# A two-layer decoder trunk on one core: a reordered opening, and softmax over a block's eight heads one block behind the scores

## The chip, the cores and the metric

The kernel runs on one core of one Trainium2 chip, in one launch. The metric is device time in microseconds (us), the median of several runs. The engines are TensorE (PE, matrix products, with PEld for its weight loads), VectorE (DVE), ScalarE (ACT), GpSimd (POOL) and SyncE (SP), on whose queue most DMAs are issued.

## What is computed

Two layers, each with a token mixer and a dense feed-forward part, on 1024 tokens of width 1024, in float32. The mixer projects to queries (8 heads of 64), keys and values (2 heads) and a pooling branch; attention looks at the own block of 128 tokens and the one before, with a sink per head:

```python
mod = c_act @ ada_w[l] + ada_b[l]                       # shift, scale, gate of both halves
h = rms_norm(x, g_pre_mix[l]) * (1.0 + scale_m) + shift_m
proj = h @ w_in[l] + b_in[l]                            # q 512, k 128, v 128, u 512 columns
...
k_cat = jnp.concatenate([jnp.pad(kb, pad)[:, :-1], kb], axis=2)    # previous block, own block
scores = jnp.einsum("bnqkgd,bnskd->bnkgqs", qb, k_cat) * (HEAD_DIM ** -0.5)
valid = (diff[None] >= 0) & (diff[None] < WINDOW) & (key_abs >= 0)
scores = jnp.where(valid[None, :, None, None], scores, NEG_INF)
probs = jax.nn.softmax(jnp.concatenate([scores, sink], axis=-1), axis=-1)[..., :-1]
out = jnp.einsum("bnkgqs,bnskd->bnqkgd", probs, v_cat)
...
mix = jnp.concatenate([attn_out, pool_out], axis=-1) @ w_out[l]
x = x + gate_m * rms_norm(mix, g_post_mix[l])
# then h = modulated rms_norm(x); x = x + gate_f * rms_norm((silu(h @ w_gate) * (h @ w_up)) @ w_down)
```

Block 0 has no block before it: the half of its scores that falls there is masked.

## The kernel before, in words

Every float32 operand of a dense product is split into a high and a low part (`split`: ACT casts the high part, L215; DVE subtracts for the low part, L216), and a product is three PE products (`mm3`, L255, L258, L259): high by high, high by low, low by high. Tokens are worked in two halves of 512 (four tiles of 128). The tile framework's planner sets each engine's order from the order of issue, the dependences and its own costs; `after` adds an order on one engine. `run` interleaves generators step by step: a main stream of dense work and streams beside it.

The opening, layer 0, half 0: x is loaded on SP's queue; the scale and shift columns of the first norm come from `ada_w[0]` in four blocks of two k (a k is 128 columns of the model width). Block 0 is a product of PE with one row as result (`ada_first_row`, L355); blocks 1 to 3 are eight weighted sums on DVE each (`ada_first_sum`, L346, L348). `ada_first_ab` (L364, L370) turns a sum into columns; `first_pieces` transposes the normalised x (L519), scales and shifts on ACT (L512) and splits. `q_pass` (four accumulator banks, 12 products of 512 columns per k) and `kv_pass` (12 of 256 per k) consume the pieces k by k. The mean squares are made on ACT (L476), the reciprocal root in small DVE steps (L266 to L273). The rotary tables are made on DVE after the last sums (L196 to L207).

Attention, `attention(h, ...)`, is a generator that runs beside the dense work (half 0 beside the u, key/value and query passes of half 1; half 1 beside the output projection of half 0 and the u pass). A group is one key head of one block (four query heads). Per group: `att_queries` (split, four transposes L798, copy L803), `att_scores` twice (four products L813, L814; two masked maxima on DVE, L816), `att_softmax` (four short DVE steps L828, L831, L836, L837; four exponentials L835 on ACT; three scalings on DVE, L841, one on ACT, L843), `att_probs` twice (four transposes L851 and a split), `att_values` twice. A group's softmax comes after the next group's queries; its probabilities come between the next group's scores. Score tiles are two (tag sb), each for one group. Beside all this runs a stream of ada weights (`ada_sum`, L287, L289, two `ar` buffers) for the rest of the layer's modulation.

Of the kernel before, what the change touches and what calls it, by code (L numbers as in the profile page):

```python
# [11 lines left out]
F32 = mybir.dt.float32  # L12
# [8 lines left out]
P = 128  # L21
# [21 lines left out]
HALO = 16  # L43
EPS = 1e-6
# [21 lines left out]
def hybrid_decoder_kernel(  # L66
# [36 lines left out]
        mix=dict(cfa=2, cfb=2, qkv=6, bqkv=1, uT=4, pt=2, vz=5, rt=1, qT=1, pth=2, pwh=1, pwl=1),  # L103
# [38 lines left out]
    make_identity(nc, eye)  # L142
    ones_r = const.tile([P, 1], F32R, name="ones_r")
# [4 lines left out]
    nc.vector.tensor_copy(ident_r, eye)  # L148
# [10 lines left out]
    mask = const.tile([P, 2, 2 * P], F32, name="mask")  # L159
    nc.gpsimd.memset(mask, 0.0)  # L160
    fill = NEG / SCALE
    for i in range(2):
        nc.gpsimd.affine_select(
            out=mask[:, i, :], in_=mask[:, i, :], pattern=[[-1, 2 * P]], compare_op=ALU.is_ge,
            fill=fill, base=P, channel_multiplier=1,
        )
        nc.gpsimd.affine_select(
            out=mask[:, i, :], in_=mask[:, i, :], pattern=[[1, 2 * P]], compare_op=ALU.is_gt,
            fill=fill, base=0, channel_multiplier=-1,
        )  # L170
    nc.gpsimd.memset(mask[:, 0, 0:P], fill)
# [4 lines left out]
    for g, w in enumerate(WINDOWS):  # L176
        nc.vector.tensor_scalar(rcnt[:, g, :], tpos, float(w), None, op0=ALU.min)
    nc.vector.reciprocal(rcnt, rcnt)


    nc.sync.dma_start(c_raw, c[0].rearrange("(p j) -> p j", j=KD))
    nc.scalar.activation(c_act, c_raw, AF.Silu)


    NB = S // P
    pos_i = const.tile([P, NB], I32, name="pos_i")
    nc.gpsimd.dma_start(pos_i, positions[0].rearrange("(t p) -> p t", p=P))
# [7 lines left out]
    def rotary_tables(prev):  # L195
        after(nc.vector.tensor_copy(pos_f, pos_i), prev)  # L196
# [7 lines left out]
        nc.vector.tensor_scalar(ang, ang, math.pi, -math.pi, op0=ALU.min, op1=ALU.max)  # L204
        nc.scalar.activation(sin_t, ang, AF.Sin)
        nc.vector.scalar_tensor_tensor(cos_t, ang, -1.0, ang, op0=ALU.mult, op1=ALU.max)
        nc.vector.tensor_scalar(cos_t, cos_t, -1.0, math.pi / 2.0, op0=ALU.mult, op1=ALU.add)  # L207
        nc.scalar.activation(cos_t, cos_t, AF.Sin)
# [4 lines left out]
    def split(hi, lo, src):  # L213

        nc.scalar.activation(hi, src, AF.Copy)  # L215
        recent["split"] = nc.vector.tensor_sub(lo, src, hi.bitcast(F32))  # L216
# [44 lines left out]
    def rsqrt_mean(ss, n):  # L261
# [8 lines left out]
        for _ in range(3):  # L270
            nc.vector.scalar_tensor_tensor(z, y, -0.5, a, op0=ALU.mult, op1=ALU.mult)
            nc.vector.tensor_mul(z, z, y)
            nc.vector.scalar_tensor_tensor(y, z, 1.5, y, op0=ALU.add, op1=ALU.mult)  # L273
# [36 lines left out]
    def load_cols(l):  # L310
        rows = t_("rows", [P, P])[:NROW]
        r = 0
        for src, n in (
# [3 lines left out]
            (nc.sync if l else nc.scalar).dma_start(rows[r : r + n, :], src.rearrange("(r p) -> r p", p=P))  # L317
            r += n
        bank = msc_bank()
# [5 lines left out]
    CW = 2 * P  # L325

    def ada_first_load(n0):

        src = ada_w[0].rearrange("(p j) n -> p j n", j=KD)
        tags = {0: ("cfa",) * 2, 1: ("cfb",) * 2, 2: ("sa", "sa", "sb", "sb"), 3: ("cfa",) * 2}[n0 // CW]  # L330
        nj = KD // len(tags)
        ws = []
        for i, tag in enumerate(tags):
            w = t_(tag, [P, nj, 2, CW])
            for m, part in enumerate((1, 0)):
                c0 = part * D + n0
                nc.sync.dma_start(w[:, :, m, :], src[:, i * nj : (i + 1) * nj, c0 : c0 + CW])
            ws += [w[:, j].rearrange("p m n -> p (m n)") for j in range(nj)]
        return ws

    def ada_first_sum(acc, ws, js):

        for j in js:
# [3 lines left out]
            else:  # L347
                last = nc.vector.scalar_tensor_tensor(acc, ws[j], c_, acc, op0=ALU.mult, op1=ALU.add)  # L348
        return last

    def ada_first_row(ws):

        bank = msc_bank()
# [1219 lines left out]
```

## Time and profile before

| | |
|---|---|
| median of three runs | 1914.03 us (1912.49 to 1915.56) |
| the profiled execution, its own time | 1912.51 us |
| its span, first to last instruction | 1910.7 us |
| mean granted TensorE clock | 0.997 |
| HBM read and written | 267.25 and 72.89 MB |

The page's first part gives each engine's busy time; a busy PE is not PE at its peak, so a window's busy time is set against its length and against the number of records. A line of a timeline gives start, length (of all records that it merges), engine, line, operation, what it writes and reads, and in brackets how long the engine stood idle before it and what released it. A group line gives busy time and mean ns of one, then the idle time before its instructions.

### The profile page before, as it was taken

What the parts mean: (1) busy time and instruction counts of PE and PEld (TensorE: products, weight loads), DVE (VectorE), ACT (ScalarE), POOL (GpSimd) and SP (SyncE); (2) the same over time, 40 slices, a digit from 0 to 9 for tenths busy, and PEclk for the clock granted to TensorE, in tenths of its full rate; (3) what the DMA queues carried; (4) which work ended last, traced back from release to release, by engine and by line L of the source; (5) the groups of instructions that cost most, each with busy time, mean ns of one, the idle gap of its engine ahead of it and who ended that gap; (6) DMA issues with size and microseconds to landing.
All of it is one profiled execution on the core that took longest, in us unless ns stands there. A gap on an engine that the chain in (4) does not pass through costs nothing.

```text
span 1910.7 us, 26084 instructions
## 1 busy us (share of the span) xinstructions
PE 1866.3 (98%) x8978; PEld 1539.2 (81%) x8978; DVE 1545.1 (81%) x2898; ACT 950.5 (50%) x1789; POOL 26.8 (1%) x84
## 2 busy tenths in 40 slices
PE   6999999999999999999999989999999999999997
PEld 4887788888888888888888868888888887888886
DVE  5999886668898888788879998846889888877687
ACT  4876795653222223445548667845622222244452
POOL 1000000000000000000000000000000000000000
PEclk9999999999999999999999999999999999999999
DMA  9355563555655665944554464536654565574342
GB/s 324 115 155 153 163 226 122 186 177 183 204 179 189 208 207 178 323 137 145 183 168 128 133 183 165 177 110 208 215 188 150 198 209 202 197 252 150 115 152 102
DMA packets 227428, 341.86 MB, mean 179 GB/s; under 512 B 16952, under 2 KB 124360, under 8 KB 227296
## 3 DMA queue, kind: packets, MB, share of 16 engines
q1 hardware_dynamic: 227152, 340.17, 54.2%
q8 instruction: 70, 1.15, 0.2%
q14 instruction: 62, 0.51, 0.1%
q0 software_dynamic: 32, 0.00, 0.0%
q10 hardware_dynamic: 112, 0.04, 0.0%
HBM read 267.25 MB, written 72.89 MB: 178 GB/s over the span
## 4 chain that ended last, share of the span: by engine, by line
PE 79%; DVE 11%; DMA 5%; ACT 3%; issue 1%; SPq 0%; DVEq 0%; ACTq 0%
PE acc L255 24%; PE acc L258 24%; PE acc L259 24%; DMA ar<-in_ada_w_dram 2%; DVE lo L216 2%; DVE ada L289 2%; PE msc L851 1%; PE msc L519 1%; ACT hi L215 1%; DMA raw<-in_w_up_dram 1%; PE pv L255 1%; DVE ph L216 1%; DMA ar<-x 1%; DVE sb L816 1%; PE pv L258 1%
## 5 line engine op out<-in xcount | busy, mean ns | idle before, releaser
L215 ACT ACTIVATE hi<-raw 128x1024 fp32r<-128x1024 f32 (+1 forms) x388 | 332.4, 869 | 365.8 <-PE acc L258 196.2
L216 DVE TENSOR_TENSOR lo<-raw,hi 128x1024 fp32r<-128x1024 f32 (+1 forms) x388 | 380.0, 986 | 123.6 <-ACT hi L215 122.8
L255 PE MATMUL acc<-t,hi 128*128 128x512 f32 x704 | 274.6, 390 | 1.5 <-ACT hi L215 1.5
L258 PE MATMUL acc<-t,hi 128*128 128x512 f32 x704 | 274.0, 389 | 0.0
L259 PE MATMUL acc<-t,lo 128*128 128x512 f32 x704 | 271.9, 389 | 0.0
L255 PE MATMUL acc<-bh,hi 128*128 128x512 f32 x520 | 202.8, 390 | 0.0
L259 PE MATMUL acc<-bh,lo 128*128 128x512 f32 x520 | 202.4, 389 | 0.0
L255 PE MATMUL acc<-hT,hi 128*128 128x512 f32 x480 | 189.7, 395 | 0.6 <-DVE fn L638 0.6
L258 PE MATMUL acc<-hT,hi 128*128 128x512 f32 x480 | 188.4, 392 | 0.0
L259 PE MATMUL acc<-hT,lo 128*128 128x512 f32 x480 | 187.7, 392 | 0.0
L1107 DVE TENSOR_TENSOR fn<-acc,fn 128x512 f32<-128x512 f32 x220 | 150.2, 683 | 37.4 <-PE acc L259 37.4
L255 PEld LDWEIGHTS acc<-t,hi 128*128 128x128 f32 x704 | 132.2, 188 | 30.8 <-ACT hi L215 3.9
L259 PEld LDWEIGHTS acc<-t,lo 128*128 128x128 f32 x704 | 132.2, 188 | 29.0 <-DVE lo L216 1.5
L258 PEld LDWEIGHTS acc<-t,hi 128*128 128x128 f32 x704 | 132.2, 188 | 27.2
L258 PE MATMUL acc<-ph,hi 128*128 128x512 f32 x320 | 124.6, 389 | 0.0
L1043 ACT ACTIVATE fn<-fn 128x512 f32<-128x512 f32 x44 | 27.8, 633 | 180.3 <-DVE fn L1107 180.3
L289 DVE SCALAR_TENSOR_TENSOR ada<-ar,c_act,ada 128x512 f32<-128x512 f32 x140 | 104.6, 747 | 12.0 <-DMA ar<-in_ada_w_dram 11.0
L259 PEld LDWEIGHTS acc<-bh,lo 128*128 128x128 f32 x520 | 97.6, 188 | 20.4
L255 PEld LDWEIGHTS acc<-bh,hi 128*128 128x128 f32 x520 | 97.6, 188 | 20.0
L255 PEld LDWEIGHTS acc<-hT,hi 128*128 128x128 f32 x480 | 90.2, 188 | 18.9 <-DVE fn L638 1.4
L259 PEld LDWEIGHTS acc<-hT,lo 128*128 128x128 f32 x480 | 90.1, 188 | 18.2
L255 PE MATMUL acc<-hi 128*128 128x512 f32 x256 | 101.1, 400 | 2.8 <-DVE fn L638 1.6
(315 smaller groups left out, 3834.6 us busy)
## 6 DMA issues: line engine op xcount, KB each, us to landing
ar<-in_ada_w_dram SPq DMA_DIRECT2D x160, 256.0 KB
raw<-in_w_gate_dram SPq DMA_DIRECT2D x44, 512.0 KB
raw<-in_w_up_dram SPq DMA_DIRECT2D x44, 512.0 KB
raw<-in_w_in_dram SPq DMA_DIRECT2D x80, 256.0 KB
raw<-keeps SPq DMA_DIRECT2D x40, 512.0 KB
keeps<-fn SPq DMA_DIRECT2D x66, 256.0 KB
two_b<-in_w_down_dram SPq DMA_DIRECT2D x30, 512.0 KB
raw<-keepa SPq DMA_DIRECT2D x25, 512.0 KB
```

Of the source, the lines that this page charges most:

```text
L215: nc.scalar.activation(hi, src, AF.Copy)
L216: recent["split"] = nc.vector.tensor_sub(lo, src, hi.bitcast(F32))
L255: ins = nc.tensor.matmul(dst, lh, rh, start=first, stop=False)
L258: nc.tensor.matmul(dst, lh, rl, start=False, stop=False)
L259: return nc.tensor.matmul(dst, ll, rh, start=False, stop=last)
L289: ins = nc.vector.scalar_tensor_tensor(acc, w, c_act[:, i : i + 1], acc, op0=ALU.mult, op1=ALU.add)
L519: ins = nc.tensor.transpose(bank[:, t * P : (t + 1) * P], src[t], ident)
L816: nc.vector.tensor_tensor_reduce(out=s[:, ii, :], in0=bank[:, ii * 2 * P : (ii + 1) * 2 * P], in1=mask[:, min(blk, 1), :], scale=SCALE, sc ...
L851: nc.tensor.transpose(bank[:, i * P : (i + 1) * P], s[:, ii, ck * P : (ck + 1) * P], ident)
L1043: nc.scalar.activation(g, g, AF.Silu)
L1107: nc.vector.tensor_add(halves_of(dst)[m], bank, halves_of(src)[m])
```

## The change

The opening: x is loaded by four DMAs on ACT's queue ahead of the ada weights; the row and position loads move, too. The ada blocks are now of 1, 1, 2, 2 and 2 k (`FIRST_BLOCKS`); the first two are row products on PE, the others sums on DVE. Half of the mean squares are made on DVE. x is scaled in three pieces of columns (128, 128, 768), each with an order behind named instructions. The rotary angles and the counts of the pool are made on DVE before the mean squares; only the two sines stay behind. The second block's pieces are issued in the middle of the first query products.

Attention: softmax is made for the eight heads of a block at once, in two steps (exponentials; scalings), after the next block's keys; scores go to three tiles in turn; probabilities come between the next block's scores, group by group. For block 0 scores, softmax, probabilities and values leave out the 128 columns of the missing block, and the cleared keys and values of it go. Buffers: qkv 5 instead of 6, pth 1 instead of 2, vz 6 instead of 5. In the dense work of half 1 the query pass comes before key/value.

```diff
-        mix=dict(cfa=2, cfb=2, qkv=6, bqkv=1, uT=4, pt=2, vz=5, rt=1, qT=1, pth=2, pwh=1, pwl=1),
+        mix=dict(cfa=2, cfb=2, qkv=5, bqkv=1, uT=4, pt=2, vz=6, rt=1, qT=1, pth=1, pwh=1, pwl=1, sc=1),
...
+    x0 = []
+    for t in range(NT):
+        x0.append(t_("fn", [P, D]))
+        nc.scalar.dma_start(x0[t], x[0, t * P : (t + 1) * P, :])
     nc.scalar.activation(c_act, c_raw, AF.Silu)
...
+    FIRST_BLOCKS = (
+        (0, 1, ("cfa",), 4), (1, 1, ("cfa",), 4), (2, 2, ("cfb",) * 2, 4),
+        (4, 2, ("sa", "sa", "sb", "sb"), 2), (6, 2, ("cfa",) * 2, 4),
+    )
...
+    def square_sum_v(ss, t, i, src, junk):
+        ins = nc.vector.tensor_tensor_reduce(
+            out=junk, in0=src, in1=src, scale=1.0, scalar=0.0, op0=ALU.mult, op1=ALU.add,
+            accum_out=ss[:, 2 * t + i : 2 * t + i + 1],
+        )
+        after(ins, ident_made)
...
-    def q_pass(l, hT, par, qkvs, ask):
+    def q_pass(l, hT, par, qkvs, ask, first=None):
...
                 mm3(banks[t], hi[:, tiles[t]], lo[:, tiles[t]], wh, wl, k == 0, k == KD - 1)
+                if first and k == 0 and t == 1:
+                    first()
...
+    def att_seen(blk):
+
+        return slice(0 if blk else P, 2 * P)
...
-    def att_softmax(n, sts, mx, nsink):
...
+    def att_softmax(blk, sts, mx, nsink):
+
+        nm = t_("st", [P, 8])
+        es = t_("st", [P, 8])
+        sm = t_("st", [P, 8])
+        nc.vector.scalar_tensor_tensor(nm, mx, -1.0, nsink, op0=ALU.mult, op1=ALU.min)
+        nc.vector.tensor_sub(es, nm, nsink)
         nc.scalar.activation(es, es, AF.Exp)
...
+        seen = [sts[i // 2][:, i % 2, att_seen(blk)] for i in range(NH)]
+        for i, sl in enumerate(seen):
             nc.scalar.activation(sl, sl, AF.Exp, bias=nm[:, i : i + 1], accum_out=sm[:, i : i + 1])
+        yield
         nc.vector.tensor_add(es, es, sm)
         nc.vector.reciprocal(es, es)
...
+        for i, sl in enumerate(seen):
+            if i % GRP < GRP - 1:
                 nc.vector.tensor_scalar(sl, sl, es[:, i : i + 1], None, op0=ALU.mult)
             else:
                 nc.scalar.activation(sl, sl, AF.Copy, scale=es[:, i : i + 1])
...
+        for t in range(NT + 1):
             cur = None
...
             if prev:
-                pblk, pt, pn, sts, mx = prev
-                att_softmax(pn, sts, mx, nsink)
-                yield
-            for u in range(GRP // 2):
+                pblk, pt, psts, pmx = prev
+                yield from att_softmax(pblk, psts, pmx, nsink)
+            for n in range(NKV):
                 if cur:
...
+                    qT = att_queries(n, qkvs[t])
+                    both = t_(("sb", "sb", "sc")[count % 3], [P, GRP // 2, 2, 2 * P])
+                    count += 1
+                    yield
+                for u in range(GRP // 2):
+                    if cur:
+                        cur[2].append(both[:, u])
+                        att_scores(blk, n, u, qT, cur[3], both[:, u])
+                    flush()
+                    if prev:
+                        late.append((pblk, n, u, att_probs(pblk, psts[n * GRP // 2 + u]), cat, pt))
+                    yield
...
     acc = ada_first_row(wss[0])
...
+    rotary_angles()
+    rstd = stats(xs, t_("rs", [P, 8]), junk=t_("pth", [P, 512]))
+    FIRST_COLS = (slice(0, P), slice(P, 2 * P), slice(2 * P, D))
+    scaled = normalise(xs, rstd, cs=FIRST_COLS[0], hold=(recent["row"], recent["hot"]))
...
     first_pieces(0)
+    acc = ada_first_row(wss[1])
...
+    queries0 = q_pass(0, hts[0], par, qkvs0, ask_q, second_piece)
+    normalise(xs, rstd, cs=FIRST_COLS[1], hold=recent["hold"])
...
+            if b == 0:
+                normalise(xs, rstd, cs=FIRST_COLS[2], hold=rest)
+            elif b + 1 < NB0:
+                last = ada_first_sum(acc, wss[b + 1], range(KD * i // nk, KD * (i + 1) // nk))
...
             yield from u_pass(l, 0, hts[0], cols, uts[0], piece_read, ask)
+            yield from q_pass(l, pieces, par, qkvs[1], ask)
             yield from kv_pass(l, pieces, par, qkvs[1], ask)
-            yield from q_pass(l, pieces, par, qkvs[1], ask)
```

## Rows read from the trace of the kernel before

**Rows 1.** The page: busy time, share of the span and instructions of each engine; then the chain of work that ended last, by engine.

```profile
PE 1866.3 (98%) x8978; PEld 1539.2 (81%) x8978; DVE 1545.1 (81%) x2898; ACT 950.5 (50%) x1789; POOL 26.8 (1%) x84
...
PE 79%; DVE 11%; DMA 5%; ACT 3%; issue 1%; SPq 0%; DVEq 0%; ACTq 0%
```

**Rows 2.** The windows: stretch, its length, busy time and records of PE, PEld, DVE, ACT and POOL, granted clock, DMA share, GB/s.

```profile
0.00:27.20 27.20, 12.42 (x37) 3.90 (x37) 9.13 (x36) 13.30 (x27) 5.12 (x21) 1.00 0.97 319
27.20:60.00 32.80, 32.72 (x198) 28.82 (x199) 29.63 (x70) 18.49 (x39) 3.54 (x6) 1.00 0.79 270
60.00:100.00 40.00, 40.00 (x241) 33.74 (x240) 37.22 (x127) 32.03 (x73) 0.27 (x2) 1.00 0.35 101
100.00:215.00 115.00, 109.75 (x643) 90.94 (x642) 109.08 (x299) 80.18 (x207) 2.86 (x12) 1.00 0.56 165
215.00:290.00 75.00, 73.12 (x420) 61.06 (x419) 63.79 (x184) 66.06 (x159) 2.80 (x8) 1.00 0.56 186
290.00:1010.00 720.00, 718.93 (x3271) 594.65 (x3270) 574.58 (x848) 306.69 (x478) 5.06 (x13) 1.00 0.56 185
1010.00:1050.00 40.00, 38.38 (x252) 32.92 (x251) 36.50 (x104) 34.49 (x84) 2.00 (x7) 1.00 0.48 145
1050.00:1165.00 115.00, 109.29 (x606) 89.78 (x605) 102.67 (x285) 75.27 (x192) 3.03 (x9) 0.99 0.53 158
1165.00:1230.00 65.00, 63.43 (x371) 53.66 (x371) 56.09 (x161) 59.09 (x142) 2.15 (x6) 1.00 0.54 183
1230.00:1900.00 670.00, 668.09 (x2955) 549.73 (x2953) 519.16 (x761) 263.83 (x396) 0.00 (x0) 1.00 0.52 175
```

**Rows 3.** The chain of work that ended last, from 100 to 215 us, by line.

```profile
by line: DMA ar<-in_ada_w_dram 20.1%; DVE ada L289 12.6%; DVE lo L216 7.1%; DMA raw<-in_w_in_dram 5.6%; PE acc L258 5.1%; PE acc L259 4.7%; PE acc L255 4.3%; DVE sb L816 3.9%; DVE ph L216 3.8%; DVE pt L947 3.2%; PE msc L851 2.3%; issue 2.3%
```

**Rows 4.** The waits of PE from 100 to 215 us: what waited for what, us in total, times, longest.

```profile
PE msc L774 <- DVE hi L769: 2.1, 1, 2.1
PE msc L387 <- ACT ph L215: 0.5, 1, 0.5
```

**Rows 5.** The timeline of the opening: start, length, engine, line, operation, in brackets the idle time before and its releaser.

```profile
10.53 0.63 ACT L476 ACTIVATE junk<-fn 128x512 bf16<-128x512 f32 x1 [0.55 <-DMA fn<-in_x_dram]
...
13.61 9.38 PE L355 MATMUL msc<-cfa,c_act 128*1 128x512 f32 x16 [6.72 <-DMA cfa<-in_ada_w_dram]
...
14.41 2.19 ACT L503 ACTIVATE fn<-fn,rs 128x1024 f32<-128x1024 f32 x2 [2.40 <-DVE rs L273]
...
22.92 0.66 PE L519 MATMUL msc<-ident,fn 128*128 128x128 f32 x4
...
23.67 1.05 PE L364 MATMUL msc<-ones_r,ar 1*128 1x1 f32 x8
...
25.20 1.45 ACT L512 ACTIVATE uT<-msc,colp 128x512 f32<-128x512 f32 x2 [1.59 <-DVE colp L375]
...
27.22 0.50 PE L255 MATMUL acc<-hi,hT 128*128 128x512 f32 x1 [1.47 <-ACT hT L215]
```

**Rows 6.** The windows again (columns as in rows 2), around the row product of the opening and around 1138 us. The clock column has no record of the time before 18.4 us and prints 1.00 there.

```profile
13.60:18.30 4.70, 4.69 (x6) 0.72 (x7) 2.65 (x7) 3.36 (x4) 0.00 (x0) 1.00 1.09 369
18.40:23.00 4.60, 4.60 (x12) 0.83 (x11) 0.70 (x2) 0.00 (x0) 0.00 (x0) 1.00 1.10 353
1133.00:1137.90 4.90, 2.69 (x11) 1.26 (x9) 4.90 (x9) 3.02 (x6) 0.00 (x0) 1.00 0.48 150
1138.00:1141.30 3.30, 3.20 (x8) 2.52 (x9) 3.14 (x10) 2.28 (x9) 0.00 (x0) 0.50 0.55 161
```

**Rows 7.** The timelines of PE and DVE from 33 to 57 us: the columns of the second ada block, the first dense products of k=2, two weighted sums, and the first and last step of the rotary angles.

```profile
33.68 0.95 PE L364 MATMUL msc<-ones_r,ar 128*128 128x1 f32 x8
...
37.66 1.19 PE L255 MATMUL acc<-hi,hT 128*128 128x512 f32 x4
...
42.22 1.54 DVE L348 SCALAR_TENSOR_TENSOR ar<-cfa,c_act,ar 128x512 f32<-128x512 f32 x2
...
51.41 0.16 DVE L196 CAST pos_f<-pos_i 128x8 f32<-128x8 int32 x1
...
56.31 0.20 DVE L207 TENSOR_SCALAR cos_t<-cos_t 128x64 f32<-128x64 f32 x1
```

**Rows 8.** The DMA issues of the first 100 us: the positions, KB, median us from issue to landing.

```profile
pos_i<-in_positions_dram POOLq DMA_DIRECT2D x1, 4.0 KB, 7.3
```

**Rows 9.** The timeline of PE: two score products of block 0, one behind the other.

```profile
73.81 0.28 PE L813 MATMUL msc<-sa,qT 128*128 128x256 f32 x1
73.93 0.28 PE L814 MATMUL msc<-sa,qT 128*128 128x256 f32 x1
```

**Rows 10.** The whole chain in order of time: start, length, what, number. Seven probability transposes.

```profile
288.31 0.77 PE msc L851 x7
```

**Rows 11.** The groups of DVE and of ACT from 64 to 215 us, shapes kept apart: busy us of all, mean ns of one, idle us before them and what ended it.

```profile
L816 DVE CUSTOM_DVE_ANT_0 sb<-msc,mask 128x256 f32<-128x256 f32 x44 | 17.2, 414 | 0.5 <-PE msc L814 0.2
...
L216 DVE TENSOR_TENSOR ph<-msc,pth 128x512 fp32r<-128x512 f32 x19 | 13.0, 685 | 1.0 <-ACT pth L215 0.9
...
L828 DVE SCALAR_TENSOR_TENSOR st<-st,sk 128x4 f32<-128x4 f32 x11 | 1.7, 154 | 0.0
...
L835 ACT ACTIVATE sb<-sb,st 128x256 f32<-128x256 f32 x44 | 21.8, 503 | 1.1 <-DVE st L828 1.1
...
L215 ACT ACTIVATE hi<-raw 128x512 fp32r<-128x512 f32 x31 | 19.1, 631 | 4.0 <-issue 2.1 <-PE acc L259 1.6 <-PE acc L258 0.4
```

More of the change, by code (lines that the diff above doesn't have):

```diff
@@ L43 @@
 HALO = 16
+UW = 576
 EPS = 1e-6
@@ L142, in hybrid_decoder_kernel @@
     make_identity(nc, eye)
+    NB = S // P
+    pos_i = const.tile([P, NB], I32, name="pos_i")
+    nc.gpsimd.dma_start(pos_i, positions[0].rearrange("(t p) -> p t", p=P))
     ones_r = const.tile([P, 1], F32R, name="ones_r")
@@ L333, in ada_first_load @@
         for i, tag in enumerate(tags):
[L334 to L337, printed above, removed]
+            w = t_(tag, [P, nj, 2, cw])
+            for j in range(0, nj, step):
+                for m, part in enumerate((1, 0)):
+                    c0 = part * D + k0 * P
+                    nc.sync.dma_start(
+                        w[:, j : j + step, m, :], src[:, i * nj + j : i * nj + j + step, c0 : c0 + cw]
+                    )
             ws += [w[:, j].rearrange("p m n -> p (m n)") for j in range(nj)]
@@ L348, in ada_first_sum, with ada_first_ab @@
                 last = nc.vector.scalar_tensor_tensor(acc, ws[j], c_, acc, op0=ALU.mult, op1=ALU.add)
+            after(last, recent["summed"])
+            recent["summed"] = last
         return last
     def ada_first_row(ws):
[L353 to L363 removed]
+        bank = msc_bank()[0:1, : ws[0].shape[1]]
+        for j in range(KD):
+            nc.tensor.matmul(bank, c_act[:, j : j + 1], ws[j], start=j == 0, stop=j == KD - 1)
+        row = t_("ar", [P, 512])[0:1, : ws[0].shape[1]]
+        recent["row"] = nc.scalar.activation(row, bank, AF.Copy)
+        return row
+    def ada_first_ab(b, acc, cols, ab):
+        k0, nk = FIRST_BLOCKS[b][:2]
+        bank = msc_bank()
+        for i in range(2 * nk):
             nc.tensor.matmul(
@@ L864, in att_values @@
         ph, pl = probs
-        for ck in range(2):
+        first = 0 if blk else 1
+        for ck in range(first, 2):
             vh, vl = attn["v", blk - 1 + ck]
@@ L868, in att_values @@
             cs = slice(ck * 2 * P, (ck + 1) * 2 * P)
-            opening = n == 0 and u == 0 and ck == 0
+            opening = n == 0 and u == 0 and ck == first
             closing = n == NKV - 1 and u == 1 and ck == 1
@@ L1357, in hybrid_decoder_kernel @@
                 layer_rows(0, par)
-        if b + 1 < NB0:
+        if 0 < b < NB0 - 1:
             first_pieces(b + 1)
-        next(keys0)
+        if (k0 + nk) % 2 == 0:
+            next(keys0)
     normalise(xs1, rstd1)
-    rotary_tables(last)
+    rotary_tables(recent["cast"])
     def ada_jobs(l):
```

238 lines of the change are left out of this document (109 added, 129 removed).

## The prediction

> **What bounds the kernel now.** I read the page first. TensorE (PE) is busy for 98% of the span, and the chain that ended last is 79% PE [rows 1]: to gain, the change must take work from PE or close gaps on it. Next come the windows [rows 2], in which PE's busy time is set against each stretch. The gaps stand in two places. In the first 27.2 us PE is busy for 12.4, and none of that is the dense work that the rest of the time consists of. In the four stretches with attention (100 to 290 and 1010 to 1230) it falls short by 5.25, 1.88, 1.62, 5.71 and 1.57 us, 16.0 together. From 27 to 100 and in the 1390 us of the other stretches it falls short by 3.1 us. In the two stretches with the large shortfall VectorE (DVE) is busy for 109.1 and 102.7 of 115 us, and the chain of the first runs through the stream of ada weights (its DMA 20.1%, its sums 12.6%) [rows 3]: in them DVE and that stream set the pace. The largest single waits of PE there are for DVE's key split (2.1 us) [rows 4].
>
> The opening is read from its timeline [rows 5]. The last quarter of x is squared from 10.53; the first ada block lands by 13.61, and PE then makes its row product (L355) in 16 records until 22.9; transposes, the columns (L364), ACT's scaling and the cast follow, and the first dense product runs at 27.22. DMA is at 0.97 of its time and 319 GB/s until then [rows 2]: bytes, not issue, decide when things land.
>
> **Part 1, the opening.** Before the first row product the kernel loads x (2.1 MB) and an ada block of 2.1 MB; the new block is 1.05 MB. 4.3 MB at 319 GB/s are 13.5 us, as seen [rows 5]; 3.2 MB are 10 us, with a start of about 1 us 11. x now goes by ACT's queue beside the ada block on SP's; both share the same bandwidth, so I let both land at 11. The row product has half the columns: 16 records that take 0.43 us each at the low pace and 0.21 at the high one. In the trace 6 records of 512 columns took 4.70 us first and 12 took 4.60 later [rows 6], so the pace doubles about 4.7 us after PE begins. Here that leaves 11 records in 4.7 us and 5 in 1.1: 16.8. Copy, columns and adds: 23.67 to 25.20 is 1.5 for eight columns' records [rows 5], I take 0.9. The second block's row product (3.4 us at the high pace) is issued before the dense work, so PE is free at about 21.2. The other road to the first product is x: squares (half on DVE now) to 12, the 2.4 us for which ACT waits on the reciprocal root [rows 5], 128 columns of scaling, transposes, scaling and cast, about 16.5 in all.
>
> In that road now stand the rotary angles, which ran from 51.4 to 56.5 on DVE in the cover of PE's dense work [rows 7], and the counts: some 5 us, behind positions whose DMA took 7.3 us to land [rows 8] and now starts at about 1.7. If DVE does them ahead of its squares, the squares start at 14 instead of 11 and the road ends near 21. So the first dense product comes at about 21.3, between 19 and 25, instead of 27.2.
>
> That is not yet the gain. With one column block (12 products at 0.23 us: one alone is 0.50 [rows 5], four in a row 1.19 [rows 7]), a second one that must wait for its own row, and the key/value pass of both (24 of 0.12), PE is fed until about 31. The third block (k=2) needs 2.1 MB more, which land after 6.8 MB, at about 21.5, and then eight sums on DVE, 5.5 us without anything between (two take 1.54 [rows 7]), 8 with the four splits that fall among them. Its columns come at about 30, and from the columns' start to the dense product it was 33.68 to 37.66, 4.0 us, partly behind other products [rows 7]; I take 2.7. So k=2 starts at about 32.7 against 37.66: **5.0 us** are left. From there the old steady run is unchanged: blocks of two k, about 10 us each on PE, with DVE freed of the angles. Bounds: 1 us (DVE's order and PE at the low pace) to 8 us (sums straight behind the landing, k=2 at 29.7).
>
> *A rule against this part.* The row shows that PE started at half pace, and that it fell to a granted clock of 0.50 (1.2 GHz) at 1138, after 4.9 us in which PE was busy for only 2.69 [rows 6]. The Trainium skill, page "TensorE: Matmul & The Clock Gate", Part 1, says that the default state is the throttled one and that activity releases it. By that rule a short row product followed by waiting lets the clock fall again; this trace has one such fall, so the rule stands as a rival below, with the time that it gives.
>
> **Part 2, block 0 of each layer.** The first block has no earlier keys, and the change leaves their columns out. Values: 12 of 24 products of 256 columns vanish, 0.12 us each [rows 9], 1.4. Probability transposes: 8 of 16, at 0.11 (seven in 0.77) [rows 10], 0.9. The score products go from 256 to 128 columns, but 128 columns are paced at 0.11 too, so 16 of them save 0.1 in all. Sum 2.4 us of PE, twice: **4.8 us**. In the first layer block 0 lies at 68 to 98, where PE has no gap [rows 2], so the saving counts there; in the second it lies at the 1010 stretch, with a shortfall of 1.62 in 40. Bounds 2.4 to 4.8. The cleared key columns on GpSimd go too; nobody waited for them.
>
> **Part 3, softmax by block.** Of the four short DVE steps (L828 0.154 us and its three like) each block now has one set instead of two: 16 fewer per half, 2.5 us; four halves, 10 us of DVE. In block 0, eight masked maxima and four splits are halved: 256 columns are worth 0.27 us between L816 (0.414) and the split (0.685) [rows 11], so 8 x 0.13 + 4 x 0.27, with the scalings 2.5 us, twice. That is relief of 15 us on the engine that limits the two long stretches. What PE gets is bounded by the shortfall of 16.0 us; the stream's own DMA waits are untouched, and in the other stretches DVE has room already. I take a little under a quarter, **3.5 us** (bounds 0 and 9).
>
> Costs. ACT now does eight exponentials in a row: 44 of them took 21.8 us, 0.50 each [rows 11], so 4.0 us instead of twice 2.0. Behind them in ACT's queue stand the casts of the next weights, the casts of probabilities and of queries, for which PE waits. The cover is ACT's lead: 1.6 of the 4.0 us that it idled before weight casts were waits for PE to release the buffer [rows 11], and a step of dense work is 12 x 0.23 = 2.7 us plus its share of attention. A further 2.0 us in 16 blocks is 32 us if none is covered, 0 if all is; nearest are the bursts of four in this trace, behind which PE's longest wait for a cast in 100 to 215 is 0.5 us [rows 4], once in four blocks; I take 0.12 per block: 2 us. The second half's query pass now comes before key/value: four accumulator banks at once after the u pass, two right behind the queries' bias adds on a busy DVE: 0.5 us (0 to 3). One buffer instead of two for the probabilities' high parts: the cast waits for the products before it, which PE issues ahead of the transposes anyway: 0.5 (0 to 3). The third score tile is what lets a new block's scores start while the old block's two tiles are still read; without a run it is worth nothing by itself. Costs together **3 us**.
>
> **Sum.** -5.0 - 4.8 - 3.5 + 3.0 = -10.3 us against the profiled execution's 1912.5 us (its span is 1910.7): 1902.2. The median of the three timed runs is 1914.0, 1.5 above the profiled one; on its scale the forecast is 1903.7.
>
> **The rivals.**
> *Forecast* (0.50): 1897 to 1909. For it: each term is PE time in a stretch in which PE is dense or late.
> *Slower: the burst of exponentials starves PE* (0.14). Place: each of the 16 blocks, PE in front of a weight or probability cast. The gains less the small costs are 12.3 us, so it decides from 0.77 us per block. At 1.2 us per block the sum is -13.3 + 1 + 19.2 = +7: 1921. For it: ACT is busy for 66 of 75 us in 215 to 290. Against: ACT's lead.
> *Given back* (0.15): the opening keeps 1 to 2 us, because DVE's angles and the third block's sums stand in the way, and the ada stream still paces 100 to 215 and 1050 to 1165, so that shorter attention turns into waits for its DMA: about -2, 1912.
> *Cold clock* (0.08): PE falls to half pace between the row products and the dense work. In the fall at 1138, 8 products took 3.3 us instead of 1.8 [rows 6]; a row product of 3.4 us at half pace and 12 dense ones cost 3.4 + 2.4, more than the 5.0 gained; attention keeps the rest: about 1909.
> *More than forecast* (0.13): the opening gains 8, and the shortfall falls by 9 us with covered bursts: -8 - 4.8 - 9 + 1 = -20.8, 1893.
> That the change does not do what it says is possible only for the order: the planner may issue blocks' steps as before; that is the second rival's price.
>
> **How the numbers follow.** The likeliest case gives 1903.5. About 0.2% (3.8 us) is what a measurement of this kernel can tell from no change. Faster: 0.50 + 0.13 + 0.08 = 0.71; same 0.15; slower 0.14. The range takes the forecast, most of the two gains beside it and the given-back case: 1890 to 1915; outside it are the slower case and the lower end of the largest gain.
>
> **What would show it.** The first dense product at 19 to 25 us and k=2's at about 32.7, with a wait of 1 to 2 us ahead of it; PE records fewer by 40 (24 value products and 16 transposes); PE's shortfall in the attention stretches down from 16 to about 12.5 before costs; no wait of PE for weight casts behind eight exponentials. The forecast is wrong if k=2 starts after 36, or if PE's waits for ACT casts grow by more than 10 us over the two layers.

## The result, and the profile after

The changed kernel takes 1924.33 us (median of four runs, 1922.73 to 1925.99), the kernel before 1914.20 beside it (1912.49 to 1915.56): a ratio of 1.0049, 95% interval 1.0036 to 1.0061. It is slower by 9.4 us (0.0049 of 1914.2), where 10.3 less were forecast. The profiled execution took 1922.73 us, its span is 1920.9.

The page of the changed kernel, engines and chain as in [rows 1], and below it the mean granted clock of its TensorE, which was 0.997 in the kernel before:

```profile
PE 1869.5 (97%) x8954; PEld 1541.5 (80%) x8954; DVE 1537.4 (80%) x2849; ACT 942.2 (49%) x1770; POOL 25.0 (1%) x67
...
PE 81%; DVE 9%; DMA 5%; ACT 3%; issue 1%; SPq 0%; DVEq 0%; ACTq 0%; POOL 0%; POOLq 0%
...
core 0: 1920.9 us, clock 0.991
```

Read against [rows 1]: the span grew by 10.2 us; PE is idle for 51.4 us of it instead of 44.4 (+7.0) and busy for 3.2 us more, though it has 24 records fewer. The clock says why it is busy for longer: 0.006 of a span of some 1920 us, about 11 us (the third decimal is rounded: 10 to 13), went into running at the lower of the two clock levels. So the work itself did shrink, by about 8 us (6 to 10), and idle time and half pace took back 18. That holds for these two executions. Over all timed ones the mean clock was 0.991 to 0.993 in the changed kernel (four, mean 0.992) and 0.993 to 0.998 in the kernel before (118, mean 0.995), so half pace is worth some 6 us of the 9.4.

Where: the windows, columns as in [rows 2], with the attention stretches cut at times that suit the later end of this kernel.

```profile
0.00:27.20 27.20, 15.20 (x67) 7.80 (x67) 17.51 (x76) 11.09 (x24) 3.83 (x17) 1.00 0.99 335
27.20:60.00 32.80, 32.53 (x197) 28.76 (x198) 27.68 (x59) 20.40 (x43) 0.22 (x2) 1.00 0.76 274
...
100.00:215.00 115.00, 108.60 (x597) 88.15 (x595) 103.83 (x264) 73.90 (x186) 3.73 (x7) 0.97 0.57 170
215.00:300.00 85.00, 78.95 (x446) 66.50 (x445) 64.61 (x179) 65.55 (x159) 1.69 (x7) 0.96 0.47 159
...
1010.00:1050.00 40.00, 39.51 (x233) 33.36 (x233) 35.23 (x115) 35.69 (x87) 1.73 (x6) 1.00 0.48 145
1050.00:1170.00 120.00, 114.42 (x646) 93.77 (x645) 107.04 (x282) 77.55 (x190) 6.24 (x7) 0.97 0.52 156
1170.00:1245.00 75.00, 68.79 (x383) 57.74 (x383) 56.21 (x152) 58.75 (x142) 2.65 (x7) 0.95 0.50 164
```

PE's shortfall in the attention stretches is 6.40, 6.05, 0.49, 5.58 and 6.21 us, 24.7 together where 16.0 stood before. Nearly all the growth is in the two stretches where a layer's last attention steps run beside the u pass and the first weight products (215 to 300: 1.88 before; 1170 to 1245: 1.57 before), and their clock is 0.96 and 0.95, where [rows 2] has 1.00. The two long stretches, with about as much shortfall as before, fall to 0.97.

The waits of PE in the changed kernel from 100 to 300 us, and the longest in layer 1 from 1050 to 1245 us (columns as in [rows 4]):

```profile
PE acc L263 <- ACT hi L220: 3.1, 1, 3.1
PE msc L892 <- DVE sb L881: 2.7, 1, 2.7
PE acc L263 <- DVE fn L680: 2.3, 3, 0.8
...
PE acc L263 <- ACT hi L220: 3.2, 1, 3.2
PE msc L892 <- DVE sb L881: 2.7, 1, 2.7
PE acc L263 <- DVE fn L680: 2.4, 3, 1.1
```

Three waits come back in both layers. In layer 0 each is followed by products at half pace; in layer 1 the last one is not. The windows around them in layer 0, and around the last one in layer 1, show it (columns as in [rows 2]):

```profile
189.00:193.50 4.50, 2.15 (x7) 0.87 (x5) 4.36 (x10) 3.52 (x9) 0.00 (x0) 0.81 0.62 183
193.50:198.00 4.50, 4.50 (x11) 3.12 (x12) 4.42 (x14) 3.81 (x14) 0.00 (x0) 0.50 0.43 122
...
260.00:263.40 3.40, 0.32 (x4) 0.12 (x2) 0.61 (x2) 1.13 (x2) 0.98 (x3) 1.00 0.44 156
263.40:267.40 4.00, 4.00 (x11) 3.12 (x12) 2.39 (x5) 3.27 (x11) 0.00 (x0) 0.57 0.67 198
286.00:290.60 4.60, 4.60 (x26) 3.88 (x26) 4.47 (x11) 3.57 (x11) 0.00 (x0) 1.00 0.00 2
290.60:293.75 3.15, 0.41 (x3) 0.03 (x1) 2.02 (x6) 3.15 (x12) 0.00 (x0) 1.00 0.00 0
293.75:298.50 4.75, 4.75 (x20) 4.17 (x21) 4.43 (x10) 4.13 (x7) 0.00 (x0) 0.64 0.25 81
...
1234.50:1237.65 3.15, 0.43 (x2) 0.01 (x2) 1.78 (x6) 3.15 (x12) 0.00 (x0) 1.00 0.00 0
1237.65:1242.40 4.75, 4.56 (x26) 3.81 (x27) 4.65 (x10) 4.16 (x7) 0.00 (x0) 1.00 0.23 74
```

- **189 to 198, the column change.** The output projection passes from its first 512 columns to its second, and its four evictions (L680) stand on DVE behind a lump: a block's rotation, the maxima of its scores, the ada sums. PE idles for 2.35 us and then has 11 records in 4.5 us. The kernel before had this in layer 1 alone [rows 6].
- **260 to 267, the first weight products.** PE waits for a weight cast, and ACT for the DMA of that weight (the last fence of this section).
- **290 to 298, the last block.** ACT's exponentials run from 288.65 to 292.7 us without a gap, then DVE scales six of the eight heads, and only behind the first of these scalings can PE transpose. The timeline of ACT, DVE and PE there (columns as in [rows 5]; the first and the last exponential, the reciprocal, the scalings, the transposes and the product behind them):

```profile
288.65 0.50 ACT L875 ACTIVATE sb<-sb,st 128x256 f32<-128x256 f32 x1
...
292.19 0.49 ACT L875 ACTIVATE sb<-sb,st 128x256 f32<-128x256 f32 x1
...
293.01 0.20 DVE L878 RECIPROCAL st<-st 128x8 f32<-128x8 f32 x1
293.25 1.67 DVE L881 TENSOR_SCALAR sb<-sb,st 128x256 f32<-128x256 f32 x6
...
293.75 1.03 PE L892 MATMUL msc<-ident,sb 128*128 128x128 f32 x5 [2.74 <-DVE sb L881]
294.43 0.77 PE L263 MATMUL acc<-hT,hi 128*128 128x512 f32 x1
```

Idle for 2.74 us, and 0.36 of the next 4.75 us lost to the clock, 1.7 us: 4.4 us in layer 0. In layer 1 the wait is as long (2.75 us), but the clock behind it stays at 1.00, with 26 records in 4.75 us instead of 20: 7.2 us in both layers together. The transposes stood at the head of PE's queue, and the weight products behind them came only after them, at 294.43.

The opening did come earlier. From the timeline of PE: the first dense product, and k=2's first; and from DVE's the last eviction of the first query projection, 60.59 us against 64.06 in the kernel before.

```profile
22.18 0.50 PE L263 MATMUL acc<-hi,hT 128*128 128x512 f32 x1
...
34.85 0.50 PE L263 MATMUL acc<-hi,hT 128*128 128x512 f32 x1
...
60.59 0.68 DVE L752 TENSOR_TENSOR qkv<-acc,bqkv 128x512 f32<-128x512 f32 x1
```

The readings below rest on three more lines: the first step of the rotary angles and DVE's first square (from its timeline), and the wait of ACT at 260 us.

```profile
6.79 0.17 DVE L196 CAST pos_f<-pos_i 128x8 f32<-128x8 int32 x1 [5.38 <-DMA pos_i<-in_positions_dram]
...
10.95 0.69 DVE L515 CUSTOM_DVE_ANT_0 pth<-fn 128x512 f32<-128x512 f32 x1
...
ACT hi L220 <- DMA raw<-in_w_up_dram: 2.9, 1, 2.9
```

### The profile page after: what moved, and what is told of

It reads as the page before. It is cut to its first block, busy times and chain, and to the rows that moved or that the text cites. A ratio compares the mean times of both kernels' runs of the same rounds, so it can differ in the third digit from the quotient of the medians.

```text
span 1920.9 us, 25974 instructions
## 1 busy us (share of the span) xinstructions
PE 1869.5 (97%) x8954; PEld 1541.5 (80%) x8954; DVE 1537.4 (80%) x2849; ACT 942.2 (49%) x1770; POOL 25.0 (1%) x67
## 4 chain that ended last, share of the span: by engine, by line
PE 81%; DVE 9%; DMA 5%; ACT 3%; issue 1%; SPq 0%; DVEq 0%; ACTq 0%; POOL 0%; POOLq 0%
PE acc L263 25%; PE acc L266 25%; PE acc L267 25%; DMA ar<-in_ada_w_dram 3%; DVE lo L221 2%; DVE ada L298 1%; DMA raw<-in_w_up_dram 1%; PE msc L892 1%; PE msc L561 1%; PE pv L263 1%; ACT hi L220 1%; PE pv L266 1%; PE msc L855 1%; PE pv L267 1%; PE msc L856 1%
## 5 line engine op out<-in xcount | busy, mean ns | idle before, releaser
L263 PE MATMUL acc<-hT,hi 128*128 128x512 f32 x480 | 193.3, 403 | 7.0 <-ACT hi L220 6.3
L266 PE MATMUL acc<-hT,hi 128*128 128x512 f32 x480 | 190.1, 396 | 0.0
```

Of the source, the lines that this page charges most:

```text
L263: ins = nc.tensor.matmul(dst, lh, rh, start=first, stop=False)
L266: nc.tensor.matmul(dst, lh, rl, start=False, stop=False)
```

## The experiments

Ratios are to the kernel before on the same chip, with 95% intervals. 0.0020 is 3.8 us. Each trace is one execution, up to 5 us from the median of its kernel (e17): prices are taken from the ratios, and the traces tell what waits for what.

### The halves of the change, and two remedies

Three theories. A: in the second half a fixed number of attention steps (16, then 10) runs beside the output projection and the u pass; the new attention has 40 steps instead of 35, so 14 are left for the first weight products instead of 9. B: the last block's lump of exponentials. C: the opening.

**e1_counts**: the steps that are left, back to a share as before.
```diff
-        run(out0, 2 * KD, (side, 4 * ADA), (att, 16))
+        run(out0, 2 * KD, (side, 4 * ADA), (att, 19))
...
-        run(u_pass(...), KD, (att, 10), (pre, NT + 2 + KD))
+        run(u_pass(...), KD, (att, 13), (pre, NT + 2 + KD))
```


> The changed kernel with two numbers altered: of the attention of the second half, 19 steps instead of 16 run beside the output projection and 13 instead of 10 beside the u pass. Theory A (the fixed step counts were right for 35 steps of a half and leave too much attention for the few up products now that a half has 40 lighter steps; PE runs dry at 260 and 290 us and again at 1203 and 1235): most of the 10 us lost per layer behind the first output projection comes back, 1908 us, between 1904 and 1914, and the gaps of 3.1 and 2.7 us go. Theory B (the burst of eight exponentials of the last block, with nothing beside it, is the cause by itself): 1920 to 1925, the 2.7 us gaps stay. Theory C (the opening is at fault): no change, 1924.

**e2_att_only**: the kernel before with the attention, buffers and order of the change, and the old opening. **e3_open_only**: the kernel before with the opening alone. Both are cuts of the diff in front.

> The kernel before with the attention part alone (softmax by block, three score tiles, block 0 cut, query pass ahead of key/value), and the old opening. Theories A and B: the attention part carries the whole loss, and without the 3.9 us that the opening gave it is 1928 us, 1925 to 1931. Theory C: it is faster than before, about 1908.

> The kernel before with the new opening alone; attention as before (the row length of two small tiles as before, too, for room). Theories A and B: the opening keeps its 3.9 us to the end, 1910 us, 1908 to 1912. Theory C: 1914 or more. If the gain is given back in the stretch from 100 to 215 us, where DVE and the ada stream set the pace: 1914.

**e4_tail_split**: the changed kernel; the last block of a half takes its softmax by key head.
```diff
-                yield from att_softmax(pblk, psts, pmx, nsink)
+                if cur:
+                    yield from att_softmax(pblk, psts, pmx, nsink)
             for n in range(NKV):
+                if not cur:
+                    yield from att_softmax(pblk, psts, pmx, nsink, range(n * GRP, (n + 1) * GRP))
...
-    ATT_STEPS = NT * (NKV * GRP // 2 + NKV + 1) + NT * 2 + NKV * GRP // 2
+    ATT_STEPS = NT * (NKV * GRP // 2 + NKV + 1) + NT * 2 + NKV * GRP // 2 + 2
```


> The changed kernel, with the softmax of the last block of each half made by key head, four heads at a time, each ahead of its own probabilities. Theory B: the waits of 2.7 us for the scalings at 291 and 1235 us, and the half-pace products after them, go: 8 us less, 1916. Theory A: 1 to 4 us less, 1920 to 1923, since the gap of 3.1 us at 260 and the shifted work stay.

Measured: e1 1926.20 (1.0055, 1.0039 to 1.0072); e2 1925.99 (1.0053, 1.0038 to 1.0068); e3 1915.78 (1.0003, 0.9994 to 1.0013); e4 1934.28 (1.0102, 1.0083 to 1.0120). The attention (with its buffers and its order of passes) carries the whole loss, and the opening alone gains nothing: C falls. As a remedy A fails, and the waits of PE in e1 from 100 to 300 us say how:

```profile
PE acc L263 <- DVE fn L680: 2.8, 3, 1.2
PE acc L263 <- ACT hi L220: 2.4, 3, 1.1
PE msc L855 <- ACT qT L840: 1.9, 3, 0.9
PE acc L267 <- DVE lo L221: 1.4, 1, 1.4
...
PE msc L892 <- DVE sb L881: 0.8, 1, 0.8
```

The wait behind the last block fell from 2.7 to 0.8 us, and no single wait for a weight's cast is above 1.1, but the steps moved to the output projection made waits there: for evictions, low parts and the queries' copies. e4 took the 2.7 us away as well; in their place PE waits 2.2 us for the cast of the high parts (`pth`, now one buffer) in both layers, and its mean clock is the lowest of all (0.991 over its four executions, 0.995 in the kernel before beside them). What else made it slower isn't shown.

### Small lumps, block 0, order, and fewer steps

**e5_by_head**: the changed kernel, still a block behind, but each key head's softmax in one step between that head's queries and scores, as before.
```diff
-                yield from att_softmax(pblk, psts, pmx, nsink)
             for n in range(NKV):
                 if cur:
...
                     yield
+                if prev:
+                    yield from att_softmax(pblk, psts, pmx, nsink, range(n * GRP, (n + 1) * GRP))
```


> The changed kernel, still a whole block behind the scores, with the same step counts, but the softmax of the block behind taken in two parts of four heads, each between the queries and the scores of one key head, as the kernel before did it (exponentials and scalings in one step). Theory G (the grain: eight exponentials, eight scalings and a block of scores in one lump leave ScalarE and VectorE late for the projections' evictions and casts, and the last block without filler): about 1916, with the idle time of TensorE in the second half's attention back near that of the kernel before. Theory M (the lag of a block itself, through the share of the attention's steps that is left when the projections' work ends: 14 of 40 against 9 of 35): stays at 1923 to 1927. Theory K (fewer tiles for the projected rows and the probabilities, and the swapped order of the two projections): stays at 1922 to 1926.

**e6_block0**: the kernel before with `att_seen` in scores, softmax, probabilities and values, and nothing else. **e7_order_bufs**: the kernel before with the lines below (the order of the passes and of the loads of their weights). **e8_before_late**: the kernel before with `(att, 16)` set to `(att, 13)`.
```diff
-        mix=dict(cfa=2, cfb=2, qkv=6, ... pth=2, pwh=1, pwl=1),
+        mix=dict(cfa=2, cfb=2, qkv=5, ... pth=1, pwh=1, pwl=1),
...
-            + all_rows(u_rows, l) + all_rows(kv_rows, l, 2) + all_rows(q_rows, l)
+            + all_rows(u_rows, l) + all_rows(q_rows, l) + all_rows(kv_rows, l, 2)
...
+            yield from q_pass(l, pieces, par, qkvs[1], ask)
             yield from kv_pass(l, pieces, par, qkvs[1], ask)
-            yield from q_pass(l, pieces, par, qkvs[1], ask)
```


> The kernel before with one part of the change alone: block 0's products, transposes, casts and exponentials over the keys that don't exist are left out (and the mask's second copy, the zero values and the zero keys with them). The prediction's term for this was 4.8 us. If the term is right and nothing gives it back: 1909 to 1911. If the time of the second half's attention is set by VectorE, ScalarE and waits rather than by TensorE's work there: 1913 to 1916, since block 0 lies in the first half of layer 0 and layer 1. No theory of the loss (G, M, K) expects it slower than 1916; if it is, the loss comes from any shift of the schedule (theory S).

> The kernel before with the queries projected ahead of the keys and values, five tiles for the projected rows where there were six, and one tile for the probabilities' high parts where there were two; the attention is as before. Theory K (these are the loss): 1920 to 1926. Theories G and M: 1914 to 1917.

> The kernel before with one number changed: beside the first half's output projection 13 steps of the second half's attention are run where there were 16, so that 12 of 35 steps (34 per cent, about what the changed kernel leaves) stay for the work after the u pass, where 9 of 35 did. Theory M (the share left over is the loss): 1919 to 1924, with about 5 us more in the stretch of the first weight products in each layer. Theories G and K: 1914 to 1917. Theory S (any shift of the schedule costs some us): above 1917 too, but with the excess spread over other stages.

Measured: e5 1918.03 (1.0019, 1.0010 to 1.0027); e6 1916.37 (1.0012, 1.0003 to 1.0020); e7 1923.35 (1.0043, 1.0031 to 1.0056); e8 1925.66 (1.0060, 1.0048 to 1.0072). G holds for the larger part: small lumps give back 0.0030, some 5.7 us. (The edit also moves the softmax, from ahead of a block's queries to between a head's queries and its scores; size and place aren't told apart.) In e5 from 215 to 300 us PE no longer waits behind the last block, and its shortfall is 3.2 us instead of 6.05 (windows, then waits of PE):

```profile
215.00:300.00 85.00, 81.81 (x472) 69.61 (x471) 68.27 (x192) 70.42 (x170) 1.69 (x7) 0.98 0.53 176
...
PE acc L263 <- ACT uT L766: 2.7, 1, 2.7
PE msc L561 <- DVE fn L541: 0.2, 1, 0.2
PE pv L266 <- DVE ph L221: 0.2, 1, 0.2
```

The wait at the first weight products stays, though: 2.7 us, now for ACT's u evictions, and 3.0 in layer 1. Over the four long stretches the shortfall is 21.2 us, where the changed kernel has 24.2 and the kernel before, in the same windows, 14.4.

What we had not expected is the other three. The old kernel, old attention included, loses 11.5 us when three steps are run later (e8), 8.2 when order and buffers change (e7), and loses 2.3 when 4.8 us of PE's work, by the prediction, are taken out (e6). In e6's trace PE is busy for as long as before (1866.3 us), at a mean clock of 0.993, and idle for 49.3 us instead of 44.4. By its range K (e7, 1920 to 1926) came true as well as G, and e8 lost even more than M said (1919 to 1924); whether the changed kernel lost on these, e9, e12 and e16 ask.

### Together, and the order alone

**e9_by_head_counts**: e5 with the counts of e1. **e10_open_block0**: e3 and e6 together. **e11_order**: e7 without the line of buffers. **e12_kv_first**: the changed kernel with the keys and values first again.

> The changed kernel with the softmax by key head, and in the second half 19 attention steps beside the output projection and 13 beside the u pass (16 and 10 before), so that 8 of 40 are left for the first weight products, as 9 of 35 are in the kernel before. So far: by head 1918.0 (ratio 1.0019), counts alone 1926.2 (1.0055), the kernel before with 3 steps fewer 1925.7 (1.0060). Theory M+G (the tail wants both: a small share left over, and work in small lumps): 1911 to 1915. Theory S (every such shift moves the waits to another stage, where the lumps of VectorE meet the projections' evictions): 1916 to 1924, with the time saved in the first weight products given back in the output projection.

> The kernel before with the two parts of the change that take time off TensorE's path: the opening, and block 0's cut, with the attention one key head behind, the buffers and the order as before. The prediction's terms: 5.0 and 4.8 us; alone they gave 1915.8 (ratio 1.0003) and 1916.4 (1.0012). If the two are real savings that each lost to a chance shift of the schedule: 1906 to 1911 together. Theory S (the work left out is answered by waits of the same length): 1914 to 1918.

> The kernel before with the queries projected ahead of the keys and values in both the order of the weights and the order of the passes; buffers as before. With the buffers this cost 8.8 us (1923.4, ratio 1.0043). If the order is the cause: 1921 to 1925. If the five tiles for the projected rows or the single tile for the probabilities are: 1914 to 1917.

> The changed kernel with the keys and values projected ahead of the queries again, and nothing else. If the order costs 8 us wherever it stands: 1915 to 1917. If what it costs hangs on which attention steps and bookings stand beside it (theory S): 1920 to 1926.

Measured: e9 1918.30 (1.0018, 1.0005 to 1.0030); e10 1914.32 (1.0003, 0.9993 to 1.0013); e11 1918.46 (1.0026, 1.0013 to 1.0038); e12 1923.02 (1.0043, 1.0025 to 1.0062). e9 is no better than e5: with the steps set back to about the share that the kernel before left over, the changed kernel gains nothing, in large lumps (e1) or in small ones, and M is no remedy. The order costs 5.0 us (0.0026) on the kernel before; on the changed kernel the intervals with it and without it overlap. Order and buffers (e7) against order alone: these overlap too, so a price of the buffers isn't shown. And both savings together (e10) still save nothing.

### The collision at the column change

Theory L: a lump of DVE at a block's first step meets the evictions at 189 us. The next block's rotation is moved to the step behind the queries of the second key head, on five kernels: **e13_after_late_rot** (the changed kernel), **e14_ob0_late_rot** (e10), **e15_before_late_rot** (the kernel before) and later **e17_open_late_rot** (e3) and **e18_block0_late_rot** (e6). **e16_by_head_kv_first** is e5 with the keys and values first.
```diff
                 yield
+                if n == NKV - 1 and t + 1 < NT:
+                    att_rotary(blk + 1, qkvs[t + 1])
```
(and out of the block's first step)

> The changed kernel with the rotation of the next block (six small operations of VectorE, 1.0 us between 186.87 and 189.3 in the changed kernel) taken from a block's first attention step to the step after the queries of its second key head. Theory L (a lump of VectorE's work at a block's first step collides with the four evictions where the output projection changes columns, 2.3 us of TensorE's waits there and half-pace products after it, in each layer): 1917 to 1921. Theory S (any shift just moves the collision): 1922 to 1928.

> The kernel before with the opening and block 0's cut (1914.3, ratio 1.0003), and the next block's rotation moved to its second key head's queries. Theory L: the terms come through, 1907 to 1911. Theory S: 1912 to 1918.

> The kernel before with the next block's rotation moved to its second key head's queries, nothing else. Its trace shows the same collision in layer 1 alone (TensorE waits 0.77 and 0.79 us for VectorE at 1135 and 1136, half-pace products to 1141). Theory L: 1909 to 1913. Theory S: 1913 to 1920.

> The changed kernel with the softmax by key head (1918.0, ratio 1.0019) and the keys and values projected ahead of the queries. If the order costs its 4.4 us (on the kernel before 1918.5, ratio 1.0026) wherever the softmax is in small lumps: 1913 to 1915. If it costs nothing beside the lag of a block: 1917 to 1920.

> The kernel before with the opening (1915.8, ratio 1.0003) and the next block's rotation moved to its second key head's queries. If the opening's gain comes through once that collision is gone: 1911 to 1912. If it was not the opening that the collision swallowed: 1914 to 1916.

> The kernel before with block 0's cut (1916.4, ratio 1.0012) and the next block's rotation moved to its second key head's queries. If the cut's gain comes through once that collision is gone: 1910 to 1912. If not: 1914 to 1917.

Measured: e13 1925.11 (1.0054, 1.0040 to 1.0068); **e14 1911.76 (0.9979, 0.9968 to 0.9990)**; e15 1914.57 (1.0000, 0.9990 to 1.0010); e16 1915.46 (1.0008, 0.9996 to 1.0021); e17 1914.65 (0.9995, 0.9986 to 1.0004); e18 1912.75 (0.9988, 0.9979 to 0.9997). L falls on the changed kernel: the wait for evictions in layer 0 went from 2.3 us in three to 0.8 in one, and the time did not move; the loss has other places enough. With the small lumps of the old attention (e14) the time fell, by 0.0024 or 4.6 us against e10. The traces show only a part of that as L's: PE's wait for the output projection's evictions is 0.8 us in layer 0, where e10 had 0.7, and not among layer 1's, where e10 had 1.2. Where the rest came from isn't shown. These are waits of PE in e10 (the one named, in layer 0 and in layer 1), then in e14 (100 to 300, then 1050 to 1245 us):

```profile
PE acc L263 <- DVE fn L680: 0.7, 1, 0.7
...
PE acc L263 <- DVE fn L680: 1.2, 2, 0.8
...
PE msc L412 <- ACT ph L220: 2.5, 2, 2.1
PE pv L263 <- ACT pth L220: 1.0, 1, 1.0
PE acc L263 <- DVE fn L680: 0.8, 1, 0.8
...
PE msc L412 <- ACT ph L220: 3.2, 3, 2.0
PE msc L814 <- DVE hi L809: 2.3, 1, 2.3
```

e14 beats both kernels: 4.0 us under the kernel before, of 9.8 that the prediction's first two terms promised. e16 confirms the lumps on another footing: with the keys and values first, lumps of eight take 1.0043 (e12) and lumps of four 1.0008, 0.0035 or 6.7 us. Against e10, e16 has the lag of a block, the changed buffers, the third score tile and the larger share of steps left over; its 1.0008 and e10's 1.0003 aren't told apart, so all of these together have no price that is shown. From 215 to 300 us PE waits 2.7 us behind the last block in e12, 0.8 in e16:

```profile
PE msc L892 <- DVE sb L881: 2.7, 1, 2.7
PE acc L263 <- ACT hi L220: 1.3, 2, 1.2
...
PE acc L263 <- ACT hi L220: 1.4, 1, 1.4
PE msc L892 <- DVE sb L881: 0.8, 1, 0.8
```

That wait of 2.7 us in e12, in layer 0, is the changed kernel's over again but for the clock, which stays at 1.00 behind it, with 26 records in 4.75 us (windows, columns as in [rows 2]):

```profile
289.00:291.85 2.85, 0.12 (x2) 0.03 (x1) 1.72 (x6) 2.85 (x10) 0.00 (x0) 1.00 0.00 0
291.85:296.60 4.75, 4.58 (x26) 3.83 (x27) 4.65 (x10) 4.13 (x7) 0.00 (x0) 1.00 0.25 79
```

## Why the prediction was wrong

**Part 1, the opening.** Right in kind, off in size. The first dense product came at 22.2 us (19 to 25 said), k=2 at 34.85, not 32.7: 2.8 us earlier than in the kernel before instead of 5.0. Its columns came at 31.39 where 30 were said, the product 3.5 us behind them where 2.7 were said, and without the wait ahead of it. At the last eviction of the queries 3.5 us are left, 2.0, 2.7 and 1.1 in e3, e14 and e17, whose opening is the same. The angles ran on DVE ahead of its squares, from 6.79 to 10.9, since the positions had landed by then, and only the counts stood between them: the squares began at 10.95, not at 14. The first row product took 5.05 us from 11.40, where 5.8 from 11 were said: fewer of its 16 records ran at the low pace. PE did not fall to half pace between the row products and the dense work: the dense products are 0.23 us apart from the start. None of this came through in e3's time (1.0003).

**Part 2, block 0.** The work went: 40 records fewer, less the 16 more of the second row product, are the 24 fewer that the page shows. The step that failed is "the saving counts there". Alone it made the kernel slower (e6), and with the rotation out of the way it gave 2.3 us (e18). The work left out was PE's, and it came back as waits for DVE and ACT and as half pace: in e6's trace from 100 to 300 us PE's waits for the key split, the keys' copy and the casts of the ada rows are 2.6, 1.3 and 1.3 us, where the kernel before has 2.1, 0.5 and 0.5.

**Part 3, the relief of DVE, 3.5 us.** The step of this part that failed. DVE is busy for 7.7 us less (10.4 in e2, with the old opening; 15 were forecast), but PE's shortfall grew from 16.0 to 24.7 us instead of falling to 12.5. I had read DVE's load in the long stretches as what paces PE; the waits show that it is the moments at which DVE or ACT is late, and the change made its work come in larger lumps.

**The costs, 3.0 us.** The term that was mis-sized, and misplaced. I spread the burst over 16 blocks at 0.12 us each, in front of casts. The trace has its price at two places, the last block of each layer's second half, where no scores of a next block stand between the exponentials and the transposes that need them: 2.74 us idle in each and 1.7 at half pace behind that of layer 0, 7.2 for both. The softmax in lumps of eight costs 5.7 us (e5) to 6.7 (e12, e16) net. So the rival "the burst starves PE" was right in kind, with another place and price, and deserved more than 0.14. That its total came near (+7, 1921) is luck: it kept 13.3 us of gains that the runs don't show. My cover, ACT's lead, was absent at the end of the attention. The order, put at 0.5 us, costs 5.0 alone on the kernel before (e11); one buffer for the high parts, put at 0.5, has no price that is shown.

**The half pace** was a rival for the opening alone. It is a large part of the loss: about 11 us in the two profiled executions, behind waits in the attention stretches, and some 6 by the mean clocks of all. It is no fixed price of a wait: behind the last block it came in layer 0 and stayed away in layer 1 and, in layer 0, in e12. And it isn't needed for a loss: e1, e7 and e8 are slower by 8.2 to 11.5 us at the mean clock of the kernel before (0.995, 0.995 and 0.996 against 0.995). The Trainium skill, page "TensorE: Matmul & The Clock Gate", section "HAM oscillation — how this bites in real kernels", tells of waits for DMA after which each tile starts at the low clock. The trace agrees that the low clock can follow a wait: behind the column change products of 512 columns start 0.43 us apart, ahead of it 0.23. Here two of the three waits are for DVE, not for DMA, and not each was followed by it.

**What stays open.** Whether the size of the lump or its place costs the time. Why this schedule is worth so much as it stands: each of seven small changes to it (e3, e6, e7, e8, e10, e11, e15) came out the same or slower, the ones that take work away among them. The prices of parts don't add: block 0's cut costs 2.3 us alone and gains 2.3 with the rotation moved, the order costs 5.0 on the old attention and between 1 and 2 on the new one, the last within the intervals. That a shift moves the moments at which DVE's and ACT's lumps meet PE's needs is shown for e1, e4, e6 and e13 by their waits; for e7, e8 and e11 it is only argued. Why e4 is the slowest of all isn't settled, as it changed two things. Why e14 is faster than e10 is shown for 1.2 us of 4.6. The first weight products' wait (260 us) stands in small lumps too (2.7 us in e5, 2.9 in e9, 3.4 in layer 1 of e16), and I did not try an earlier load.

## What to carry to other kernels

In this kernel the grain of the stream that fills gaps beside dense work decided: before lumping its steps to save an idle engine's microseconds, look at its last piece, where nothing is left to stand between producer and consumer, and price the gap as a range, from its idle time alone to that and the half-paced products that may follow. With PE 97% busy by the page, a saving of PE's work did not count here until a step of DVE was moved as well (e14, e18); test each saving in more than one schedule, and not alone. And where a count of steps was set by hand for another number of steps, expect it to need setting again, though setting it to the old share may only move the wait.

## What the runs showed of the hardware

Idle stretches of PE of 2.3 to 3.1 us cost, where the clock fell, half as much to as much again in pace: behind the three of layer 0, the granted clock was 0.50 over 4.5 us, 0.57 over 4.0 and 0.64 over 4.75, which is 2.3, 1.7 and 1.7 us. It did not always fall: behind 2.75 us of idle in layer 1, and behind 2.73 in e12, it was 1.00. A busy PE hides this: its busy time grew by 3.2 us while its work shrank.
